# Forget gate's rows written into their operands in place, and first weights in smaller pieces, in a two-layer decoder trunk

## The chip, the cores and the metric

The kernel runs on one core of a Trainium2 chip. The metric is the device time of one execution in microseconds (us), as the median of several runs. The core's engines have their own instruction queues and work side by side: TensorE (PE in the rows), VectorE (DVE), ScalarE (ACT), GpSimd (POOL) and SyncE (SP), which only issues DMAs here.

## The reference

An input x of 256 tokens by 1024 features passes through two layers. All weights are float32 in memory.

```python
for layer in range(2):
    x = x + 0.5 * swiglu(rms_norm(x, norm_ffn1[layer]), ffn1 weights)      # 1024 -> 2816 -> 1024
    xn = rms_norm(x, norm_mix[layer])
    mixed = mix_stick_moba(xn, ...) if layer == 0 else mix_forget_dilated(xn, ...)
    x = x + mixed @ w_out[layer]
    x = x + 0.5 * swiglu(rms_norm(x, norm_ffn2[layer]), ffn2 weights)

def swiglu(x, w_gate, w_up, w_down):
    return (silu(x @ w_gate) * (x @ w_up)) @ w_down

def mix_forget_dilated(xn, w_in, b_f, ...):
    proj = xn @ w_in                       # q, k, v for 16 heads of 64, and 8 columns for the forget gate
    log_f = log_sigmoid(proj[..., 3072:] + b_f)
    # heads 0 to 7: q, k normed; logits = q k^T / 8 + c_i - c_j with c = cumsum(log_f); causal softmax; times v
    # heads 8 to 15: q, k normed and rotated; softmax over a dilated window of earlier keys; times v
```

## The kernel before

**Precision.** Every weight matrix is split in two after it is loaded: `hi` is a cast to fp32r on ACT, `lo` the rest, a subtraction on VectorE. Activations are split in the same way, so that each product takes three matmuls (hi by hi, hi by lo, lo by hi).

**Loading.** `unit` does this for 1 MB (or 768 KB) of weights. It takes one of the three buffers of the pool `raw`, lets SP issue the DMA, and writes two halves of hi and lo. A raw buffer comes free when the `lo` of both halves is done. SP's DMAs go in order: one that waits for a buffer holds those behind it. The first two units, the first 2 MB of the gate's weights, are loaded in two DMAs of 512 KB each, and x's second tile of 128 tokens is loaded between the two units.

**Opening.** x (two tiles of 128 tokens), the identity and the three vectors of RMS gains are loaded; TensorE transposes the gains (line 200) and x (`tt`); VectorE multiplies x by the gains (`xg`), ACT and VectorE split it into `xt`. Then come the gate's matmuls (`acc`, tokens in two tiles: 24 matmuls of 512 columns each per tile) and the up matrix's (`z`). GpSimd issues small DMAs for the head gains (`hg`) at the start.

**Mixing of layer 1.** `forget` computes the forget gate. It has the operands `ck` and `cq`, which carry the cumulated log gate as four extra rows of the second head group's product, beside rows of ones. It takes raw buffers for `wf`, `cl` (8 x 4 x 256: the two parts of c and of -c) and `rows` (zeros, ones, and the copies of `cl` by eight GpSimd DMAs), which two casts on GpSimd turn into `ck` and `cq`. At the same time the first group (dilated heads) runs its steps: `z` logits, `t` the softmax (maximum `mx` and scaling `t` on VectorE, exponential on ACT), `tt` transposes, `pT` their copies, one on VectorE and one on ACT, and `o` outputs. Between these, TensorE projects the second group's q, k and v; k1 and v1 below are the units of its k and v. `qn` are normed q or k; `rp` is the power -1/2 of a mean square (`ms`, or `hss` for heads) on GpSimd; `diag` is the identity times rp, which TensorE multiplies by ones.

**Order.** TensorE's order is written by hand: the projections are the main program and a small planner (`Weave`) inserts the other tasks by its own clock. The other engines' orders are made by the scheduler, save instructions that `keep_in_program_order` pins.

Of the kernel before, what the change touches and what calls it, by code (L numbers as in the profile page):

```python
# [16 lines left out]
P = 128  # L17
# [56 lines left out]
def bcast_rows(ap, offset, n):  # L74
    return bass.AP(tensor=ap.tensor, offset=ap.offset + offset, ap=[[0, P], [1, n]])
# [37 lines left out]
def trunk(ctx, tc, a, out):  # L113
# [69 lines left out]
    def load_x(t):  # L183
        for h in range(2):
            sl = slice(h * 512, (h + 1) * 512)
            nc.sync.dma_start(x[t][:, sl], a["x"][0, t * P:(t + 1) * P, sl])
# [5 lines left out]
        c0 = (2 * n + layer) * KT  # L192
        return gains_t[:, c0:c0 + KT]

    def load_gains():
        rows = raw_p.tile([6 * KT, P], F32, tag="raw", name="grows")
        for i, n in enumerate(("norm_ffn1", "norm_mix", "norm_ffn2")):
            nc.scalar.dma_start(rows[2 * KT * i:2 * KT * (i + 1)], a[n].rearrange("l (k p) -> (l k) p", p=P))
        tb = acc()
        nc.tensor.transpose(tb[:, :6 * KT], rows, ident[:6 * KT, :6 * KT])  # L200
        nc.vector.tensor_copy(gains_t[:, :6 * KT], tb[:, :6 * KT])

    identb = const.tile([P, P], BF, name="identb")
    negb = const.tile([P, 3, P], BF, name="negb")
# [28 lines left out]
    def unit(src, shape):  # L233

        w = raw_p.tile([P, *shape], F32, tag="raw", name=nm("raw"))
        n = shape[0] // 2
        if first_units:
            for i in range(2):
                nc.sync.dma_start(w[:, i * n:(i + 1) * n], src[:, i * n:(i + 1) * n])
            first_units.pop()()  # L240
        else:
            nc.sync.dma_start(w, src)
        parts = []
        for i in range(2):
            wi = w[:, i * n:(i + 1) * n]
            hi = spl_p.tile([P, n, shape[1]], F32R, tag="hi", name=nm("hi"))
            lo = spl_p.tile([P, n, shape[1]], F32R, tag="lo", name=nm("lo"))
            nc.scalar.copy(hi, wi)  # L248
            nc.vector.tensor_sub(lo, wi, hi.bitcast(F32))  # L249
            parts.append((hi, lo))  # L250
        return lambda k: tuple(v[:, k % n] for v in parts[k // n])

    def col_units(src, c0, width):
# [167 lines left out]
    def head_gain(src, rope, scale, i=0):  # L421

        if not rope:
            gp = hgp.tile([P, 16], F32, name=nm("hg"))[:, 0:1]
            for j in range(2):
                nc.gpsimd.dma_start(gp[j * HD:(j + 1) * HD], src.rearrange("o d -> d o"))
            if scale != 1.0:
                nc.gpsimd.tensor_scalar(gp, gp, scale, 0.0, op0=ALU.mult, op1=ALU.add)
            return gp
        g = hgp.tile([P, HD], F32, tag=f"g{i}", name=nm("hg"))  # L430
        nc.gpsimd.dma_start(g, bcast_rows(src, 0, HD))
        if scale != 1.0:
            nc.gpsimd.tensor_scalar(g, g, scale, 0.0, op0=ALU.mult, op1=ALU.add)
        gc = hgp.tile([P, 2, HD], F32, tag=f"gc{i}", name=nm("gc"))
        gs = hgp.tile([P, 2, HD], F32, tag=f"gs{i}", name=nm("gs"))
        cc = cv("cc").rearrange("p (t d) -> p t d", d=HD)
        ss = cv("ss").rearrange("p (t d) -> p t d", d=HD)
        for t in range(2):
            nc.gpsimd.tensor_mul(gc[:, t], cc[:, t], g)
            half_swap(lambda u, v: nc.gpsimd.tensor_mul(gs[:, t, u], ss[:, t, u], g[:, v]))  # L440
        return gc, gs

    def mix_gains(layer):

# [9 lines left out]
    def _mix(mp, layer, xt, gains, done):  # L454
# [55 lines left out]
        def forget():  # L510

            ck = mp.tile([P, 4, SEQ], F32R, name="ck")
            cq = mp.tile([P, 4, SEQ], F32R, name="cq")
            wf = raw_p.tile([P, KT, P], F32, tag="raw", name="wf")
            nc.gpsimd.memset(wf, 0.0)
            nc.scalar.dma_start(wf[:, :, 0:8], w[:, 3072:3080].rearrange("(k p) n -> p k n", p=P))
            bf = mp.tile([8, 224], F32, name="bf")[:, 0:1]
            nc.scalar.dma_start(bf, a["b_f"].rearrange("o h -> h o"))
            wfh = spl_p.tile([P, KT, P], F32R, tag="hi", name="wfh")
            wfl = spl_p.tile([P, KT, P], F32R, tag="lo", name="wfl")  # L520
            nc.scalar.copy(wfh, wf)
            nc.vector.tensor_sub(wfl, wf, wfh.bitcast(F32))
            pe.join(*xt.rdone)
            ps = acc()
            for k in range(KT):
                mm(ps[:, :SEQ], wfh[:, k], xt.hi[:, k], k == 0, False)
                mm(ps[:, :SEQ], wfh[:, k], xt.lo[:, k], False, False)
                mm(ps[:, :SEQ], wfl[:, k], xt.hi[:, k], False, k == KT - 1)

            def rest():  # L530
                y = mp.tile([8, SEQ], F32, tag="t1", bufs=4, name="lgy")
                e = mp.tile([8, SEQ], F32, tag="t1", bufs=4, name="lge")
                nc.vector.tensor_mul(y, ps[:8, :SEQ], xt.rb[:8])
                nc.vector.tensor_scalar(y, y, bf, None, op0=ALU.add)
                nc.scalar.activation(e, y, AF.Abs)
                nc.scalar.activation(e, e, AF.Exp, scale=-1.0)
                nc.scalar.activation(e, e, AF.Ln, bias=1.0)
                nc.vector.scalar_tensor_tensor(y, y, 0.0, e, op0=ALU.min, op1=ALU.subtract)
                yield LEAD_F
                tb = acc()  # L540
                for t in range(2):
                    nc.tensor.transpose(tb[:, 8 * t:8 * t + 8], y[:, t * P:(t + 1) * P], ident[:8, :8])
                lg = mp.tile([P, 2, 16], F32, name="lg")[:, :, 0:8]
                nc.vector.tensor_copy(lg, tb[:, 0:16].rearrange("p (t h) -> p t h", h=8))
                yield 1.0
                tb = acc()
                mm(tb[:8, 0:P], lg[:, 0], cv("le"), True)
                mm(tb[:8, P:SEQ], lg[:, 1], cv("le"), False)
                mm(tb[:8, P:SEQ], lg[:, 0], ones, False)
                ch = mp.tile([8, SEQ], F32R, tag="t1", bufs=4, name="ch")  # L550
                cl = raw_p.tile([8, 4, SEQ], F32, tag="raw", name="cl")
                nc.vector.tensor_copy(ch, tb[:8, :SEQ])
                nc.vector.tensor_copy(cl[:, 2], ch.bitcast(F32))
                nc.vector.tensor_sub(cl[:, 3], tb[:8, :SEQ], cl[:, 2])
                nc.vector.tensor_scalar_mul(cl[:, 0:2], cl[:, 2:4], -1.0)

                rows = raw_p.tile([P, 2, 4, SEQ], F32, tag="raw", name="rows")
                nc.gpsimd.memset(rows, 0.0)
                for s in range(2):
                    b0 = s * HD  # L560
                    nc.gpsimd.memset(rows[b0:b0 + 4], 1.0)
                    for i in range(2):
                        for j in range(2):
                            nc.gpsimd.dma_start(rows[b0 + 2 * i + j:b0 + 2 * i + j + 1, i],
                                              cl[s::2, 2 * i + j])
                for i, dst in enumerate((ck, cq)):
                    nc.gpsimd.tensor_copy(dst, rows[:, i])

            return (ck, cq), [pe.spawn(rest())]

# [169 lines left out]
        row_gemm(second.lhs, a["w_out"][layer], ca, 2, 2, lambda t, h, ps: done(t, h, ps, 1.0))  # L740


    load_x(0)
    nc.scalar.dma_start(ident, a["consts"][:, 0:P])
    load_gains()
    xt = Normed(gain(0, 0))

    def second_tile():
# [11 lines left out]
    for layer in range(2):  # L760
        nxt = Normed(gain(1, layer), True)
        gains = []

        def between():
            if layer == 0:
                load_consts()
            gains.extend(mix_gains(layer))

        ffn(layer, a["ffn1_w_gate"], a["ffn1_w_up"], a["ffn1_w_down"], xt, nxt.start, between)
        xt = nxt  # L770
        nxt = Normed(gain(2, layer))
# [29 lines left out]
```

## Time and profile before

| | before |
|---|---|
| time, median of 3 runs | 1043.26 us (1041.93 to 1043.9) |
| time of the profiled execution | 1043.78 us |
| its span, first to last instruction | 1042.0 us |
| TensorE busy (matmul) | 1004.4 us, 96% |
| VectorE busy | 604.9 us, 58% |
| ScalarE busy | 498.9 us, 48% |
| GpSimd busy | 98.3 us, 9% |
| read from memory | 173.99 MB |

The span is the time that the trace covers; the execution's own time is 1.78 us longer. Shares are of the span. Matmuls are pipelined, so two that run back to back overlap in the rows: a matmul's place is its start.

### The profile page before, as it was taken

The page shows a single profiled execution, that of the slowest core. Times are in us where ns is not written, and L with a number is a line of the kernel's source. Part 1 is how long each engine was busy: PE and PEld are TensorE (multiplying, and loading weights), DVE is VectorE, ACT ScalarE, POOL GpSimd, SP SyncE. Part 2 cuts the span into 40 slices and gives each one's busy share as a digit, 9 for nine tenths or more (in the row PEclk, how much of TensorE's full clock was granted, in tenths as well). Part 3 has the DMA queues.
Part 4 walks back from the last instruction along what each step waited for, and adds up shares of the span by engine and source line. Part 5 has one row for each costly group of instructions (what it writes and reads, how often), then busy time and mean ns, then how long its engine had stood idle before and what let it go on. Part 6 is the DMA issues. An engine that isn't in the chain of part 4 may idle for free.

```text
span 1042.0 us, 13509 instructions
## 1 busy us (share of the span) xinstructions
PE 1004.4 (96%) x5409; PEld 834.6 (80%) x5409; DVE 604.9 (58%) x794; ACT 498.9 (48%) x666; POOL 98.3 (9%) x109
## 2 busy tenths in 40 slices
PE   5999999999999999999999999999968899999998
PEld 3888988879777888988788899887746678889986
DVE  5654564588676554554655455458576755545541
ACT  6644554455665444543545345346344545435530
POOL 5000000064000000000000000005461000000000
PEclk9999999999999999999999999999988999999999
DMA  9664655464233654665455546534144424545631
GB/s 308 228 208 123 219 206 199 146 217 162 84 123 122 213 178 124 211 235 182 164 187 178 175 156 244 185 120 156 41 163 162 162 82 163 202 150 180 235 122 40
DMA packets 81871, 175.95 MB, mean 169 GB/s; under 512 B 4480, under 2 KB 21200, under 8 KB 81808
## 3 DMA queue, kind: packets, MB, share of 16 engines
q1 hardware_dynamic: 80000, 174.80, 49.4%
q8 instruction: 42, 0.69, 0.3%
q0 software_dynamic: 512, 0.17, 0.2%
q10 hardware_dynamic: 1296, 0.12, 0.1%
q14 instruction: 21, 0.17, 0.0%
HBM read 173.99 MB, written 1.05 MB: 168 GB/s over the span
## 4 chain that ended last, share of the span: by engine, by line
PE 89%; DVE 5%; DMA 2%; ACT 2%; issue 1%; POOL 0%; ACTq 0%; POOLq 0%
PE acc L149 55%; PE z L149 24%; PE o L149 6%; DVE lo L249 3%; PE tt L165 3%; ACT hi L248 1%; PE tt L149 1%; DMA raw<-in_ffn_w_up 1%; DMA x<-in_x 1%; DMA raw<-in_w_in_cd 1%; DVE xg L291 0%; ACT t L670 0%; DVE mx L664 0%; DVE t L674 0%; DMA ident<-in_consts 0%
## 5 line engine op out<-in xcount | busy, mean ns | idle before, releaser
L249 DVE TENSOR_TENSOR lo<-raw,hi 128x1024 fp32r<-128x1024 f32 (+1 forms) x344 | 403.0, 1183 | 247.2 <-ACT hi L248 235.9
L248 ACT CAST hi<-raw 128x1024 fp32r<-128x1024 f32 (+1 forms) x344 | 344.0, 1011 | 301.6 <-PE z L149 130.8
L149 PE MATMUL acc<-hi,xt 128*128 128x512 f32 (+1 forms) x1088 | 346.4, 388 | 5.7 <-ACT xt L292 2.5
L149 PEld LDWEIGHTS acc<-hi,xt 128*128 128x128 f32 x1088 | 205.6, 191 | 46.4 <-DVE xt L293 4.4
L149 PE MATMUL z<-hi,xt 128*128 128x512 f32 (+1 forms) x768 | 226.4, 371 | 0.0
L149 PE MATMUL acc<-lo,xt 128*128 128x512 f32 (+1 forms) x544 | 208.3, 383 | 1.8 <-DVE lo L249 1.8
L149 PEld LDWEIGHTS z<-hi,xt 128*128 128x128 f32 x768 | 142.4, 188 | 19.9
L149 PE MATMUL z<-lo,xt 128*128 128x512 f32 (+1 forms) x384 | 142.3, 371 | 0.0
L149 PEld LDWEIGHTS acc<-lo,xt 128*128 128x128 f32 x544 | 104.1, 191 | 17.7 <-DVE lo L249 2.1
L149 PE MATMUL acc<-hi,hh 128*128 128x512 f32 x264 | 103.5, 392 | 0.0
L149 PE MATMUL acc<-hi,hl 128*128 128x512 f32 x264 | 102.9, 390 | 0.0
L149 PE MATMUL acc<-lo,hh 128*128 128x512 f32 x264 | 102.8, 389 | 0.0
L227 POOL TENSOR_TENSOR rp<-ms,mhalf 128x1 f32<-128x1 f32 (+1 forms) x24 | 36.7, 1527 | 637.1 <-DVE ms L225 637.0
L149 PEld LDWEIGHTS z<-lo,xt 128*128 128x128 f32 x384 | 72.1, 188 | 10.0
L392 DVE TENSOR_TENSOR h<-z,sg 128x512 f32<-128x512 f32 (+1 forms) x48 | 30.9, 643 | 53.1 <-PE z L149 53.1
L149 PEld LDWEIGHTS acc<-hi,hl 128*128 128x128 f32 x264 | 49.5, 188 | 10.4
L149 PEld LDWEIGHTS acc<-hi,hh 128*128 128x128 f32 x264 | 49.5, 188 | 10.4
L149 PEld LDWEIGHTS acc<-lo,hh 128*128 128x128 f32 x264 | 49.6, 188 | 10.0
L388 ACT ACTIVATE sg<-acc,rp 128x512 f32<-128x512 f32 (+1 forms) x48 | 31.4, 654 | 42.2 <-PE acc L149 41.6
L261 ACT CAST hh<-tt 128x512 fp32r<-128x512 f32 (+1 forms) x48 | 26.5, 552 | 44.9 <-PE tt L165 24.7
L262 DVE TENSOR_TENSOR hl<-tt,hh 128x512 fp32r<-128x512 f32 (+1 forms) x48 | 31.0, 647 | 20.3 <-ACT hh L261 19.7
L149 PE MATMUL o<-hi,hh 128*128 128x512 f32 x88 | 34.4, 391 | 0.0
(144 smaller groups left out, 806.6 us busy)
## 6 DMA issues: line engine op xcount, KB each, us to landing
raw<-in_ffn_w_down SPq DMA_DIRECT2D x44, 1024.0 KB, 5.0
raw<-in_ffn_w_up SPq DMA_DIRECT2D x32, 1024.0 KB, 5.1
raw<-in_ffn_w_gate SPq DMA_DIRECT2D x30, 1024.0 KB, 5.1
raw<-in_ffn_w_gate SPq DMA_DIRECT2D x16, 768.0 KB, 4.5
raw<-in_ffn_w_up SPq DMA_DIRECT2D x16, 768.0 KB, 4.4
raw<-in_w_in_ab SPq DMA_DIRECT2D x12, 1024.0 KB, 5.2
raw<-in_w_in_cd SPq DMA_DIRECT2D x12, 1024.0 KB, 5.2
raw<-in_w_out SPq DMA_DIRECT2D x8, 1024.0 KB, 5.1
```

The lines of the kernel that those rows point to most:

```text
L149: nc.tensor.matmul(o, lhsT, rhs, start=start, stop=stop, skip_group_check=True)
L165: nc.tensor.transpose(tb[:, b, n * HP:(n + 1) * HP], src[r, j * P:(j + 1) * P], ident[r, r])
L227: nc.gpsimd.tensor_tensor(r, m, mhalf[:, :width], op=ALU.pow)
L248: nc.scalar.copy(hi, wi)
L249: nc.vector.tensor_sub(lo, wi, hi.bitcast(F32))
L261: nc.scalar.copy(halves(hi), v)
L262: nc.vector.tensor_sub(halves(lo), v, halves(hi).bitcast(F32))
L388: nc.scalar.activation(sg[t][:, :n], pg[:, :n], AF.Silu, scale=xt.r[t])
L392: nc.vector.tensor_mul(hs[t][:, :n], pu[:, :n], sg[t][:, :n])
```

## The change

The loading of the start is written anew: the identity goes first, on SP's queue; ACT's first instruction is a load of its function table; only the gains of the first norm are loaded at the start, those of the other two just before w_down of layer 0. The first two units are loaded in four DMAs of 256 KB each, and their hi and lo are made in pieces of that size; x's second tile is loaded behind both. The head gains' DMAs are pinned in program order. In `forget`, `ck` and `cq` are set to zeros and ones by GpSimd at its start, `cl` has a buffer of its own, and the eight DMAs write straight into `ck` and `cq`; `rows`, the two casts and one copy are gone.

```diff
-    def load_gains():
-        rows = raw_p.tile([6 * KT, P], F32, tag="raw", name="grows")
-        for i, n in enumerate(("norm_ffn1", "norm_mix", "norm_ffn2")):
+    def load_gains(names):
+        rows = raw_p.tile([2 * KT * len(names), P], F32, tag="raw", name=nm("grows"))
+        for i, (n, name) in enumerate(names):
...
-        if first_units:
-            for i in range(2):
-                nc.sync.dma_start(w[:, i * n:(i + 1) * n], src[:, i * n:(i + 1) * n])
-            first_units.pop()()
-        else:
-            nc.sync.dma_start(w, src)
+        pieces = 4 if first_units else 1
+        for i in range(pieces):
+            sl = slice(i * shape[0] // pieces, (i + 1) * shape[0] // pieces)
+            nc.sync.dma_start(w[:, sl], src[:, sl])
...
-            nc.scalar.copy(hi, wi)
-            nc.vector.tensor_sub(lo, wi, hi.bitcast(F32))
+            m = min(n, 2 * n // pieces)
+            for j in range(0, n, m):
+                nc.scalar.copy(hi[:, j:j + m], w[:, i * n + j:i * n + j + m])
+                nc.vector.tensor_sub(lo[:, j:j + m], w[:, i * n + j:i * n + j + m], hi[:, j:j + m].bitcast(F32))
             parts.append((hi, lo))
+        if first_units:
+            first_units.pop()()
...
-        nc.gpsimd.dma_start(g, bcast_rows(src, 0, HD))
+        tc.keep_in_program_order(nc.gpsimd.dma_start(g, bcast_rows(src, 0, HD)))
...
+            for dst in (ck, cq):
+                nc.gpsimd.memset(dst.bitcast(F32), 0.0)
+                for s in range(2):
+                    nc.gpsimd.memset(dst[s * HD:s * HD + 4].bitcast(F32), 1.0)
             wf = raw_p.tile([P, KT, P], F32, tag="raw", name="wf")
...
-                ch = mp.tile([8, SEQ], F32R, tag="t1", bufs=4, name="ch")
-                cl = raw_p.tile([8, 4, SEQ], F32, tag="raw", name="cl")
-                nc.vector.tensor_copy(ch, tb[:8, :SEQ])
-                nc.vector.tensor_copy(cl[:, 2], ch.bitcast(F32))
-                nc.vector.tensor_sub(cl[:, 3], tb[:8, :SEQ], cl[:, 2])
-                nc.vector.tensor_scalar_mul(cl[:, 0:2], cl[:, 2:4], -1.0)
-
-                rows = raw_p.tile([P, 2, 4, SEQ], F32, tag="raw", name="rows")
-                nc.gpsimd.memset(rows, 0.0)
+
+                cl = mp.tile([8, 4, SEQ], F32R, name="cl")
+                nc.vector.tensor_copy(cl[:, 2], tb[:8, :SEQ])
+                nc.vector.tensor_sub(cl[:, 3], tb[:8, :SEQ], cl[:, 2].bitcast(F32))
+                nc.vector.tensor_scalar_mul(cl[:, 0:2], cl[:, 2:4].bitcast(F32), -1.0)
                 for s in range(2):
                     b0 = s * HD
-                    nc.gpsimd.memset(rows[b0:b0 + 4], 1.0)
-                    for i in range(2):
+                    for i, dst in enumerate((ck, cq)):
                         for j in range(2):
-                            nc.gpsimd.dma_start(rows[b0 + 2 * i + j:b0 + 2 * i + j + 1, i],
-                                              cl[s::2, 2 * i + j])
-                for i, dst in enumerate((ck, cq)):
-                    nc.gpsimd.tensor_copy(dst, rows[:, i])
+                            nc.gpsimd.dma_start(dst[b0 + 2 * i + j:b0 + 2 * i + j + 1].bitcast(F32),
+                                                cl[s::2, 2 * i + j].bitcast(F32))
...
+    nc.scalar.preload_act_table_set("silu_and_others")
+    nc.sync.dma_start(ident, a["consts"][:, 0:P])
     load_x(0)
-    nc.scalar.dma_start(ident, a["consts"][:, 0:P])
-    load_gains()
+    load_gains([(0, "norm_ffn1")])
...
-    first_units.extend([lambda: None, second_tile])
+    first_units.extend([second_tile, lambda: None])
...
             if layer == 0:
                 load_consts()
+                load_gains([(1, "norm_mix"), (2, "norm_ffn2")])
```

VectorE's first rows, before (x_81 is x's first tile, x_82 its second; raw_111 and raw_124 the first two units):

```order
L225 TENSOR_SCALAR ms_167<-ss_165 128x1
L201 COPY gains_t<-acc_98 128x48
L249 TENSOR_TENSOR lo_117<-raw_111,hi_116 128x1024
L291 TENSOR_TENSOR xg_152<-tt_135,gains_t 128x512
L291 TENSOR_TENSOR xg_156<-tt_135,gains_t 128x512
L249 TENSOR_TENSOR lo_121<-raw_111,hi_120 128x1024
L225 TENSOR_SCALAR ms_208<-ss_206 128x1
L293 TENSOR_TENSOR xt_102<-xg_152,xt_101 128x4x128
L293 TENSOR_TENSOR xt_102<-xg_156,xt_101 128x4x128
L249 TENSOR_TENSOR lo_128<-raw_124,hi_127 128x1024
L249 TENSOR_TENSOR lo_132<-raw_124,hi_131 128x1024
```

The same rows of the changed kernel (raw_110 and raw_127 are the first two units):

```order
L202 COPY gains_t<-acc_97 128x16
L226 TENSOR_SCALAR ms_178<-ss_176 128x1
L293 TENSOR_TENSOR xg_163<-tt_146,gains_t 128x512
L293 TENSOR_TENSOR xg_167<-tt_146,gains_t 128x512
L249 TENSOR_TENSOR lo_116<-raw_110,hi_115 128x512 x2
L295 TENSOR_TENSOR xt_101<-xg_163,xt_100 128x4x128
L249 TENSOR_TENSOR lo_122<-raw_110,hi_121 128x512
L295 TENSOR_TENSOR xt_101<-xg_167,xt_100 128x4x128
L249 TENSOR_TENSOR lo_122<-raw_110,hi_121 128x512
L249 TENSOR_TENSOR lo_133<-raw_127,hi_132 128x512 x2
L249 TENSOR_TENSOR lo_139<-raw_127,hi_138 128x512 x2
```

The gains' copy and xg stand ahead of every lo now, and lo goes in eight pieces with the xt between them.

ACT in the mixing of layer 1, before, from the square (`sq`) of q1's first tile on (raw_6436 and raw_6446 hold the two halves of k1's weights):

```order
L486 ACTIVATE sq_6325<-acc_6244,rp_5797 128x512
L666 ACTIVATE t_19_6361<-z_6349,mx_6359 128x128
L666 ACTIVATE t_20_6373<-z_6350,mx_6371 128x128
L682 COPY pT_6396<-tt_6383 128x384
L666 ACTIVATE t_19_6361<-z_6349,mx_6359 128x256
L666 ACTIVATE t_20_6373<-z_6350,mx_6371 128x256
L486 ACTIVATE sq_6460<-acc_6321,rp_5900 128x512
L248 CAST hi_6438<-raw_6436 128x1024
L248 CAST hi_6442<-raw_6436 128x1024
L248 CAST hi_6448<-raw_6446 128x1024
L248 CAST hi_6452<-raw_6446 128x1024
```

ACT of the changed kernel some rows earlier in the program, around the log-sigmoid (`lge`); raw_6451 and raw_6461 hold k1's weights, raw_6695 the first half of v1's:

```order
L248 CAST hi_6453<-raw_6451 128x1024
L248 CAST hi_6457<-raw_6451 128x1024
L248 CAST hi_6463<-raw_6461 128x1024
L506 ACTIVATE kT_5980<-tt_6189 128x4x128
L470 ACTIVATE v_3_6202<-acc_6167,rp_5917 128x512
L248 CAST hi_6467<-raw_6461 128x1024
L248 CAST hi_6697<-raw_6695 128x1024
L541 ACTIVATE lge<-lgy 8x256
```

k1's four casts, which stood behind the softmax of the first group's second step, now stand ahead of the log-sigmoid, and a cast of v1 with them.

GpSimd between the two diag tiles of the mixing norm of layer 1, before:

```order
L227 TENSOR_TENSOR rp_5797<-ms_5795,mhalf 128x1
L305 TENSOR_TENSOR diag_5799<-ident,rp_5797 128x128
L515 MEMSET wf 128x1024
L227 TENSOR_TENSOR rp_5900<-ms_5898,mhalf 128x1
L305 TENSOR_TENSOR diag_5902<-ident,rp_5900 128x128
```

and of the changed kernel:

```order
L228 TENSOR_TENSOR rp_5814<-ms_5812,mhalf 128x1
L307 TENSOR_TENSOR diag_5816<-ident,rp_5814 128x128
L517 MEMSET ck 128x1024
L517 MEMSET cq 128x1024
L519 MEMSET ck 4x1024 x2
L519 MEMSET cq 4x1024 x2
L521 MEMSET wf 128x1024
L228 TENSOR_TENSOR rp_5917<-ms_5915,mhalf 128x1
L307 TENSOR_TENSOR diag_5919<-ident,rp_5917 128x128
```

Six memsets have come in ahead of wf's and of the second tile's rp and diag.

## Rows read from the trace of the kernel before

**Rows 1.** The page's busy times: engine, us, share of span, instructions.

```profile
PE 1004.4 (96%) x5409; PEld 834.6 (80%) x5409; DVE 604.9 (58%) x794; ACT 498.9 (48%) x666; POOL 98.3 (9%) x109
```

**Rows 2.** TensorE's waits over the span: total us, times, longest.

```profile
PE acc L200 <- DMA x<-in_x: 9.7, 1, 9.7
```

**Rows 3.** Timeline of the opening: start, us, engine, line, operation, [idle before <-releaser].

```profile
2.14 0.45 ACTq L198 DMA_DIRECT2D grows<-in_norm_ffn  x1
...
9.67 0.31 PE L200 MATMUL acc<-ident,grows 48*128 48x48 f32 x1 [9.67 <-DMA x<-in_x]
...
11.27 1.28 DVE L291 TENSOR_TENSOR xg<-tt,gains_t 128x512 f32<-128x512 f32 x2
...
12.47 1.22 DVE L249 TENSOR_TENSOR lo<-raw,hi 128x1024 fp32r<-128x1024 f32 x1
...
13.40 0.80 PE L149 MATMUL acc<-hi,xt 128*128 128x512 f32 x1 [2.55 <-ACT xt L292]
...
21.67 1.28 ACT L388 ACT_TABLE_LOAD   x1 [0.50 <-PE acc L149]
...
27.64 0.39 PE L149 MATMUL z<-hi,xt 128*128 128x512 f32 x1
27.87 0.39 PE L149 MATMUL z<-lo,xt 128*128 128x512 f32 x1
```

**Rows 4.** DMA view, 0 to 30 us: GB/s in 40 slices; then KB, us to landing.

```profile
GB/s 0 0 109 238 379 326 107 40 192 377 392 367 331 385 396 391 377 385 385 388 410 388 385 393 382 366 393 390 388 208 104 208 396 412 352 63 3 68 180 377
...
x<-in_x SPq DMA_DIRECT2D x4, 256.0 KB, 5.3
...
ident<-in_consts ACTq DMA_DIRECT2D x1, 64.0 KB, 3.3
grows<-in_norm_ffn ACTq DMA_DIRECT2D x2, 8.0 KB, 7.4
```

**Rows 5.** Windows in layer 1's mixing; the sum is of four with PEclk 0.50.

```profile
740.00:750.00 10.00, 10.00 (x62) 7.92 (x61) 4.64 (x20) 4.12 (x9) 0.00 (x0) 1.00 0.01 2
757.00:798.31 41.31, 27.94 (x155) 20.29 (x154) 30.36 (x68) 20.43 (x30) 14.76 (x14) 0.79 0.60 204
...
791.49:798.31 6.82, 6.26 (x29) 4.47 (x29) 2.96 (x9) 2.10 (x3) 0.30 (x1) 0.50 0.71 279
sum 17.05, PE 15.89 PEld 12.18 DVE 12.00 ACT 6.54 POOL 5.77; mean PE 3.97 PEld 3.04 DVE 3.00 ACT 1.64 POOL 1.44
```

**Rows 6.** TensorE's timeline, 755 to 800 us: the five rows that waited.

```profile
758.90 0.49 PE L149 MATMUL acc<-hi,xt 128*128 128x512 f32 x1 [1.77 <-ACT hi L248]
761.16 0.79 PE L149 MATMUL acc<-lo,xt 128*128 128x512 f32 x1 [1.76 <-DVE lo L249]
...
771.23 0.69 PE L165 MATMUL tt<-ident,qn 64*128 64x64 f32 x8 [4.21 <-ACT pT L682]
...
783.40 0.46 PE L165 MATMUL tt<-ident,qn 64*128 64x64 f32 x8 [2.69 <-ACT pT L682]
...
792.05 1.11 PE L165 MATMUL tt<-ident,t 64*128 64x64 f32 x12 [2.94 <-DVE t L674]
```

**Rows 7.** Timelines of VectorE and ACT in the same stretch.

```profile
758.64 0.53 DVE L674 TENSOR_SCALAR t<-t,l 128x128 f32<-128x128 f32 x2
...
767.89 1.99 ACT L248 CAST hi<-raw 128x1024 fp32r<-128x1024 f32 x2 [8.10 <-DMA raw<-in_w_in_cd]
```

**Rows 8.** Timelines of GpSimd, 690 to 770 us, and of TensorE at 711.

```profile
695.25 0.55 POOL L227 TENSOR_TENSOR rp<-ms,mhalf 128x1 f32<-128x1 f32 x1 [172.92 <-DVE ms L225]
...
706.30 0.95 POOL L515 MEMSET wf<- 128x1024 f32 x1 [10.02 <-DMA bf<-in_b_f]
707.58 2.66 POOL L227 TENSOR_TENSOR rp<-ms,mhalf 128x1 f32<-128x1 f32 x1 [0.33 <-DVE ms L225]
...
754.48 3.69 POOL L561 MEMSET rows<- 4x2048 f32 x2
...
711.01 0.38 PE L149 MATMUL acc<-diag,ones 128*128 128x128 f32 x2
```

More of the change, by code (lines that the diff above doesn't have):

```diff
@@ L193, in gain @@
         return gains_t[:, c0:c0 + KT]
-    def load_gains():
-        rows = raw_p.tile([6 * KT, P], F32, tag="raw", name="grows")
-        for i, n in enumerate(("norm_ffn1", "norm_mix", "norm_ffn2")):
-            nc.scalar.dma_start(rows[2 * KT * i:2 * KT * (i + 1)], a[n].rearrange("l (k p) -> (l k) p", p=P))
+    def load_gains(names):
+        rows = raw_p.tile([2 * KT * len(names), P], F32, tag="raw", name=nm("grows"))
+        for i, (n, name) in enumerate(names):
+            nc.scalar.dma_start(rows[2 * KT * i:2 * KT * (i + 1)], a[name].rearrange("l (k p) -> (l k) p", p=P))
+        m, c0 = 2 * KT * len(names), 2 * KT * names[0][0]
         tb = acc()
-        nc.tensor.transpose(tb[:, :6 * KT], rows, ident[:6 * KT, :6 * KT])
-        nc.vector.tensor_copy(gains_t[:, :6 * KT], tb[:, :6 * KT])
+        nc.tensor.transpose(tb[:, :m], rows, ident[:m, :m])
+        nc.vector.tensor_copy(gains_t[:, c0:c0 + m], tb[:, :m])
     identb = const.tile([P, P], BF, name="identb")
@@ L236, in unit @@
         n = shape[0] // 2
-        if first_units:
-            for i in range(2):
-                nc.sync.dma_start(w[:, i * n:(i + 1) * n], src[:, i * n:(i + 1) * n])
-            first_units.pop()()
-        else:
-            nc.sync.dma_start(w, src)
+        pieces = 4 if first_units else 1
+        for i in range(pieces):
+            sl = slice(i * shape[0] // pieces, (i + 1) * shape[0] // pieces)
+            nc.sync.dma_start(w[:, sl], src[:, sl])
         parts = []
         for i in range(2):
-            wi = w[:, i * n:(i + 1) * n]
             hi = spl_p.tile([P, n, shape[1]], F32R, tag="hi", name=nm("hi"))
             lo = spl_p.tile([P, n, shape[1]], F32R, tag="lo", name=nm("lo"))
-            nc.scalar.copy(hi, wi)
-            nc.vector.tensor_sub(lo, wi, hi.bitcast(F32))
+            m = min(n, 2 * n // pieces)
+            for j in range(0, n, m):
+                nc.scalar.copy(hi[:, j:j + m], w[:, i * n + j:i * n + j + m])
+                nc.vector.tensor_sub(lo[:, j:j + m], w[:, i * n + j:i * n + j + m], hi[:, j:j + m].bitcast(F32))
             parts.append((hi, lo))
+        if first_units:
+            first_units.pop()()
         return lambda k: tuple(v[:, k % n] for v in parts[k // n])
@@ L425, in head_gain @@
             for j in range(2):
-                nc.gpsimd.dma_start(gp[j * HD:(j + 1) * HD], src.rearrange("o d -> d o"))
+                tc.keep_in_program_order(nc.gpsimd.dma_start(gp[j * HD:(j + 1) * HD], src.rearrange("o d -> d o")))
             if scale != 1.0:
```

## The prediction

> **What bounds the kernel now.** I read the page first: TensorE is busy for 1004.4 us, 96% of the span [rows 1]. So only some 38 us of idle TensorE, and what a low clock costs it, can be won; work taken off another engine counts only where TensorE waits for it. The list of TensorE's waits names the largest: 9.7 us at line 200, the transpose of the gains at the start [rows 2]. The other long ones lie close together in the timeline, in layer 1's mixing (below). The change touches both places.
>
> The opening comes from the timeline [rows 3]. The transposes of the gains start at 9.67 although x was asked for first. What they wait for is the gain rows: the third DMA of them is issued at 2.14 and, by the DMA view, these take about 7.4 us to land, while the identity on the same queue took 3.3 [rows 4]. The inferred releaser says x, which took 5.3 from an earlier issue; it was long there. In the same answer the transfer rate falls to 107 and 40 GB/s in the slices from 4.5 to 6 us (40 slices over 30 us), beside some 390 later; that is when the six small DMAs that GpSimd issues for the head gains are under way. From 9.67 a chain runs: xg at 11.27, first weight matmul at 13.40, first matmul of z at 27.64 [rows 3]. From there the matmuls follow 0.23 apart (27.64, 27.87), with no wait among the list's larger ones before the mixing, so what z's start gains is kept.
>
> The second place: from 757 to 798.31 TensorE is busy 27.94 of 41.31 us [rows 5]. Five waits make up the rest: 1.77, 1.76, 4.21, 2.69 and 2.94 [rows 6], 13.4 together. After such waits the granted clock is 0.50 (the lower level, 1.2 GHz) for stretches with 15.89 us of busy TensorE [rows 5]; at the higher level that is half, so 7.9 is lost to the clock. Together 21.3 us, over 20.0 of work. The cause lies in the buffers: cl and rows (whose memsets run around 754 [rows 8]) hold two of the three raw buffers, so the weights of k1's second half and v1 come late: ACT, idle for 8.10, can make the second half's hi only at 767.89 when its DMA lands, and the pT that TensorE wants stands behind those casts [rows 7]. From 740 to 750, just before, VectorE is busy 4.64 of 10 and the DMA share is 0.01 [rows 5]: room for the same work earlier.
>
> **The opening, part by part.** Gone from the start: two of three gain DMAs, six head-gain DMAs of GpSimd (now in order, far later, when nothing waits: their products are used tens of us afterwards) and the table load of 1.28 at 21.67 [rows 3], which moves to ACT's first slot, where it lies beside x's landing. But the one gain DMA left is issued behind it, at some 0.7 + 1.3 = 2.0. Landing: between 3.3 us (the identity) and 7.4 us (gains before) later [rows 4], so 5.3 to 9.4. I take 5.5: the queue that slowed it is gone and it is nearest to the identity, 16 rows from memory. The Trainium skill ("DMA: Bandwidth & Descriptors", section "Queues, rings and completion order") says that each DMA engine takes turns between the queues that have work, a packet at a time; by that the gains would not stand behind 2 MB of weights, T would be 5.3 and the opening worth -5.4, where the gains' own row gives 9.4 and -1.3. The identity's 3.3 agrees with the rule and the gains' 7.4, by itself, does not.
>
> From the gains' landing T: xg begins 11.27 - 9.67 = 1.6 later and two take 1.28 [rows 3], so T + 2.9. Then VectorE does, in its new order, eight lo pieces (128x512, half of 1.22, so 0.61 [rows 3]) and two xt of 0.64: T + 9.1. For x's second tile: two xg 1.28, an ms 0.15, an xt 0.64, two lo of 1.22 for the up weights, an xt 0.64: T + 14.2. The second token tile's last 12 matmuls need that xt: 12 x 0.227 = 2.7 (27.64 to 27.87 [rows 3]), so z starts at T + 16.9. With T = 5.5 that is 22.4, against 27.64: **-5.2**. With T = 9.4 it is -1.3; with 5.0, -5.7. Weights are not late: 2.6 MB at 390 GB/s lie before x's second tile, so it lands at some 9 to 12 us, and VectorE reaches it at 14.6.
>
> The other gains now come in layer 0 just before w_down. Their buffer waits for the mask constants; ACT is idle there, and w_down has two buffers until then. A lo more stands ahead of one h, and TensorE gets one more transpose: **+0.4** (0 to 1.2, one lo).
>
> **The mixing of layer 1.** With cl in a tile of its own, and the rows copied by DMA straight into ck and cq, no raw buffer is taken there. In the new order ACT casts k1's four halves and one of v1 before the log-sigmoid, and VectorE follows; their buffers are freed by splits done before 730, so the loads land before 745. The waits of 1.77 and 1.76 go entirely. Also gone: 128x2048 and two 4x2048 memsets (3.69 for the pair [rows 8]), two CASTs on GpSimd, one small copy on VectorE.
>
> The three later waits shrink or stay, and a new one comes, because TensorE arrives earlier while VectorE has more in hand. I laid the new rows of VectorE and ACT end to end with the old durations. The scaling of t that pair 1's transposes need ended at 758.64 + 0.53 = 759.2 [rows 7]. Now about 1.0 of shift, two lo (2.4), an hss (0.69), two mx (0.5) come ahead of it, less the copy (0.4): some 763.4. TensorE, with 12 matmuls (2.7), a z of 1.2 and no wait from 757, is there at 760.9: a wait of 2.5 to 2.9 that wasn't there; I take 2.8. In the same way the two waits for pT give 1.4 and 0.9, the next for t 3.0 (three lo ahead of it), and 0.8 goes in small ones. Sum 8.9 in place of 13.4. Two of them are near 3 us, the kind after which the clock fell for 3.41 us: 2 x 1.7 = 3.4 in place of 7.9. New length 20.0 + 8.9 + 3.4 = 32.3 against 41.3: **-9.0**. Bounds: with every wait gone -21; with as many waits as before except the first two, and the same clock, -3.5. I stay near the walk: -5 to -13. What comes behind 800 is not touched.
>
> **A new wait.** GpSimd now has six memsets (128x1024 twice, 4x1024 four times) before wf's, in order, between the gains' diag tiles. They wait for the last matmul of FFN1, about 702.3. By the pair of 4x2048, 3.69, one of 4x1024 is 0.92, and wf's 128x1024 took 0.95 [rows 8]: 7 x 0.93 = 6.5, to 708.9, where before wf's memset started at 706.30 and rp at 707.58. Behind them rp (2.66) and diag (0.40): to about 712.0. TensorE's ones-by-diag matmul stood at 711.01 [rows 8]: **+1.1** (0, if rp takes 0.55 as at 695.25, to 2). The Trainium skill ("GPSIMD Engine Reference", section "8. Key points") warns that GpSimd shares its memory interfaces with VectorE, which contends when it reads two inputs. wf's memset took 0.95 beside a VectorE that is busy throughout, so a memset doesn't show it; rp's 2.66 against 0.55 would fit. If memsets suffered like rp, the wait would be longer by some us.
>
> **Sum.** -5.2 - 9.0 + 1.1 + 0.4 = -12.7. The profiled execution took 1043.78, 0.52 above the median, so 1031.1 for it and **1030.6** for the median 1043.26. Differences within 0.2% (2.1 us) I call no change.
>
> **Rivals.** (1) The gains land no earlier (T = 9.4): for it, they go behind the table load and beside four pieces already queued; against, GpSimd's DMAs are gone. 1043.26 - 1.3 - 9.0 + 1.5 = 1034.5. (2) VectorE is the bound in the mixing: it is busy 30.36 of 41.31 there [rows 5], and only 0.4 of its work is removed. Waits stay as long as the three were, clock too: -3.5, so 1043.26 - 5.2 - 3.5 + 1.5 = 1036.1. Against it: 5 of the lo halves move ahead of 757. (3) **Slower**: the shorter waits follow one another so closely that the clock stays low over the whole mixing stretch, as it did from 791.49 to 798.31 [rows 5]. With 20.0 of work at half clock, 40 + 8.9 against 41.3 gives +7.6; with -5.2 + 1.5: +3.9, so 1047.2. It decides once 16 of the 20 us of work run low (28.9 + 16 = 45, which eats the opening's gain). Against it: the other three low stretches ended after 3.41 us. (4) The change does not do what it says: T late and the mixing's waits only renamed, 1043.26 - 1.3 - 2 + 1.5 = 1041.5.
>
> **Numbers.** Forecast 0.60 (its own range 1026 to 1034.3), rival 1 0.13, rival 2 0.15, rival 3 0.06, rival 4 0.06. The range reaches down to -18 (opening -5.7, mixing -13, no new wait) and up past rival 2: 1025 to 1038. It leaves out rivals 3 and 4 and some of the edges. Faster 0.88, no change 0.06, slower 0.06.
>
> **What would show it.** Right: line 201's transpose at 5 to 6; z's first matmul near 22.4; one table load before the first square; k1's hi and lo casts before lge; no wait on hi or lo near 757; two waits near 3 us between 755 and 785 (less the shift), each with 3.41 us at 0.50; a wait on diag of about 1 us. Wrong: gains landing at 9; a clock of 0.50 for most of the mixing; waits of 4 us there again; memsets of 1.8 us each.

## The result, and the profile after

The changed kernel takes 1029.43 us (median of 4 runs, 1028.47 to 1030.1) against 1043.53 for the kernel before beside it: a ratio of 0.9867, with a 95% interval of 0.985 to 0.9884, so 14.1 us or 1.3% faster. The forecast was 1030.6, a change of -12.7; the measured time lies 1.2 us below it, within its range. The profiled execution took 1029.01, 14.8 below that of before, with a span of 1027.2.

The page, busy times (engine, us, share of the span), as in [rows 1]:

```profile
PE 1003.0 (98%) x5410; PEld 833.3 (81%) x5410; DVE 603.3 (59%) x798; ACT 497.7 (48%) x669; POOL 87.9 (9%) x110
```

TensorE does the same work within a span that is 14.8 us shorter. Its waits over the span (us in total, times, longest), the first six of nine, against [rows 2]:

```profile
PE tt L165 <- DVE t L673: 4.7, 4, 1.6
PE z L149 <- ACT t L669: 3.9, 4, 2.3
PE acc L201 <- DMA ident<-in_consts: 2.9, 1, 2.9
PE z L149 <- ACT kT L506: 2.1, 2, 1.4
PE acc L149 <- ACT xt L294: 2.1, 1, 2.1
PE acc L149 <- DVE xt L295: 1.8, 4, 0.7
```

The 9.7 us wait for the gains is now 2.9, and no wait is longer than that. The timeline of the opening (start, us, engine, line, operation), against [rows 3]:

```profile
0.72 1.28 ACT L742 ACT_TABLE_LOAD   x1 [0.72 <-PEq L790]
...
0.76 0.40 ACTq L198 DMA_DIRECT2D grows<-in_norm_ffn  x1
...
2.85 0.28 PE L201 MATMUL acc<-ident,grows 16*128 16x16 f32 x1 [2.85 <-DMA ident<-in_consts]
...
4.27 1.36 PE L165 MATMUL tt<-ident,x 64*128 64x64 f32 x16 [1.14 <-DMA x<-in_x]
...
6.04 1.12 ACT L248 CAST hi<-raw 128x512 fp32r<-128x512 f32 x2
6.17 0.15 DVE L226 TENSOR_SCALAR ms<-ss 128x1 f32<-128x1 f32 x1 [2.82 <-ACT junk L302]
6.25 1.29 DVE L293 TENSOR_TENSOR xg<-tt,gains_t 128x512 f32<-128x512 f32 x2
...
7.07 0.61 ACT L294 CAST xt<-xg 128x512 fp32r<-128x512 f32 x1
...
7.74 0.80 PE L149 MATMUL acc<-hi,xt 128*128 128x512 f32 x1 [2.10 <-ACT xt L294]
...
9.40 1.22 PE L149 MATMUL acc<-hi,xt 128*128 128x512 f32 x2 [0.41 <-DVE xt L295]
...
18.41 0.69 DVE L295 TENSOR_TENSOR xt<-xg,xt 128x512 fp32r<-128x512 f32 x1
...
21.98 0.39 PE L149 MATMUL z<-hi,xt 128*128 128x512 f32 x1
```

The gains' transpose went from 9.67 to 2.85, z's first matmul from 27.64 to 21.98, and the opening has no table load behind 2.00. One profile fixes z's place only to some 1.4 us: in seven profiles with this opening (the change twice, and the runs below on the opening alone, the held buffers and the two orders) z's first matmul stands between 21.98 and 23.34; with the opening of before it stands at 27.64, and at 28.28 in the run of the forget part alone. The DMA view of the same 30 us (GB/s in 40 slices; KB and us to landing), against [rows 4]:

```profile
GB/s 0 0 92 238 306 352 325 333 339 371 369 358 391 380 382 404 410 401 412 401 385 382 388 391 393 390 380 380 382 393 399 126 180 385 396 336 128 158 401 412
...
ident<-in_consts SPq DMA_DIRECT2D x1, 64.0 KB, 2.1
grows<-in_norm_ffn ACTq DMA_DIRECT2D x1, 8.0 KB, 1.9
```

The dip to 107 and 40 GB/s between 4.5 and 6 us is gone (325 and 333 in its place), and the gains land 1.9 us after their issue.

In layer 1's mixing TensorE's waits are these (timeline, 738 to 784 us), against [rows 6]:

```profile
741.54 0.92 PE L149 MATMUL z<-kT,qT 64*128 64x256 f32 x8 [1.35 <-ACT kT L506]
...
758.21 0.51 PE L165 MATMUL tt<-ident,t 64*128 64x64 f32 x6 [1.27 <-DVE t L673]
...
761.30 0.69 PE L165 MATMUL tt<-ident,qn 64*128 64x64 f32 x8 [0.24 <-ACT pT L681]
...
772.34 0.46 PE L165 MATMUL tt<-ident,qn 64*128 64x64 f32 x8 [0.76 <-ACT pT L681]
...
778.34 0.60 PE L165 MATMUL tt<-ident,t 64*128 64x64 f32 x6 [1.59 <-DVE t L673]
```

The waits for hi and lo are gone, the 4.21 and 2.69 for pT are 0.24 and 0.76, the 2.94 for t is 1.59; 1.27 for t is new, and so is the 1.35 for kT. The windows at the lower clock (columns as in [rows 5]):

```profile
759.43:766.26 6.83, 6.59 (x30) 4.74 (x28) 3.77 (x16) 2.10 (x4) 0.42 (x1) 0.50 0.02 4
779.91:783.32 3.41, 3.41 (x9) 2.38 (x8) 1.35 (x3) 1.82 (x3) 0.39 (x1) 0.50 0.75 285
```

10.00 us of busy TensorE run at 1.2 GHz there, against 15.89.

Matmul by matmul, in the order of the program, the new kernel is ahead by 5.7 us at z's first matmul, 5.5 at layer 0's w_down, 4.85 from layer 0's mixing norm (210.66 before, 205.81 after) up to layer 1's mixing, 3.4 at the row at 741.54, and 15.1 once the mixing of the first group is done. The rest of the program keeps that to within 0.3 us.

### The profile page after: what moved, and what is told of

Same layout as the page of the kernel before. It is cut to its first block, busy times and chain, and to the rows that moved or that the text cites. A ratio compares the mean times of both kernels' runs of the same rounds, so it can differ in the third digit from the quotient of the medians.

```text
span 1027.2 us, 13525 instructions
## 1 busy us (share of the span) xinstructions
PE 1003.0 (98%) x5410; PEld 833.3 (81%) x5410; DVE 603.3 (59%) x798; ACT 497.7 (48%) x669; POOL 87.9 (9%) x110
## 4 chain that ended last, share of the span: by engine, by line
PE 88%; DVE 6%; ACT 2%; issue 1%; POOL 1%; DMA 1%; SPq 0%; ACTq 0%; DVEq 0%; POOLq 0%
PE acc L149 54%; PE z L149 25%; PE o L149 6%; DVE lo L249 3%; PE tt L165 3%; ACT hi L248 1%; PE tt L149 1%; POOL rp L228 1%; POOL sq L498 1%; DMA raw<-in_w_in_ab 1%; DVE mx L663 0%; ACT t L669 0%; DMA x<-in_x 0%; DVE qn L493 0%; DVE xg L293 0%
## 5 line engine op out<-in xcount | busy, mean ns | idle before, releaser
L249 DVE TENSOR_TENSOR lo<-raw,hi 128x1024 fp32r<-128x1024 f32 (+2 forms) x348 | 403.4, 1171 | 240.5 <-ACT hi L248 229.8
L248 ACT CAST hi<-raw 128x1024 fp32r<-128x1024 f32 (+2 forms) x348 | 344.6, 1001 | 293.8 <-PE z L149 124.8
L228 POOL TENSOR_TENSOR rp<-ms,mhalf 128x1 f32<-128x1 f32 (+1 forms) x24 | 31.9, 1328 | 618.8 <-DVE ms L226 618.7
```

The source lines that it names most:

```text
L228: nc.gpsimd.tensor_tensor(r, m, mhalf[:, :width], op=ALU.pow)
L248: nc.scalar.copy(hi[:, j:j + m], w[:, i * n + j:i * n + j + m])
L249: nc.vector.tensor_sub(lo[:, j:j + m], w[:, i * n + j:i * n + j + m], hi[:, j:j + m].bitcast(F32))
```

## The experiments

All were timed against the kernel before in interleaved rounds; the ratio with its interval decides.

| run | median us | ratio to before | 95% interval |
|---|---|---|---|
| the change | 1029.43 | 0.9867 | 0.985 to 0.9884 |
| the change, again | 1028.89 | 0.9859 | 0.9845 to 0.9872 |
| forget part alone | 1033.9 | 0.991 | 0.9896 to 0.9925 |
| opening alone | 1039.69 | 0.9964 | 0.9951 to 0.9977 |
| two raw buffers held | 1036.77 | 0.9933 | 0.9909 to 0.9958 |
| head gains first | 1031.03 | 0.9887 | 0.987 to 0.9903 |
| two pieces | 1030.46 | 0.9873 | 0.986 to 0.9887 |
| three gains first | 1031.17 | 0.9881 | 0.9867 to 0.9894 |
| both first | 1034.31 | 0.9907 | 0.9892 to 0.9922 |
| before, head gains late | 1041.28 | 0.9976 | 0.9967 to 0.9985 |
| xg ahead of ms | 1029.23 | 0.986 | 0.9846 to 0.9874 |
| log-sigmoid behind kT | 1024.78 | 0.9818 | 0.9802 to 0.9833 |
| both orders | 1025.0 | 0.9817 | 0.9801 to 0.9833 |

**Each part alone.** The function `forget` is exchanged whole between the two kernels:

```diff
-                cl = raw_p.tile([8, 4, SEQ], F32, tag="raw", name="cl")
+                cl = mp.tile([8, 4, SEQ], F32R, name="cl")
...
```

The first run makes this and the rest of `forget`'s edits in the kernel before; the second takes them back in the changed kernel.

> The kernel before with the forget part alone. The theory that the two parts add up, and that the mixing of layer 1 is worth about 10 us in the changed kernel's trace, expects 1033 to 1035 us (9 to 10 below 1043.5). The rival, that the mixing gains only because TensorE comes to it in another phase, expects 1038 or more.

> The changed kernel with the forget gate of before. If the parts add up, the opening is worth 5 to 5.5 us and the time is 1038 to 1039. The rival, that the earlier opening is eaten by later waits, expects 1041 or more.

The forget part gives 9.4 us (by its ratio), as expected; the opening 3.8 (2.4 to 5.1), under the 5 to 5.5 expected. Together 13.2, against 13.9 and 14.7 in the two timings of the change: they add up within their intervals. The opening's shortfall shows in its profile: z starts at 22.75, which is 4.9 ahead of before, and 3.6 is left behind the mixing norm of layer 0. The phase in which TensorE arrives at layer 1's mixing doesn't matter much: there the run keeps waits of 1.8, 1.8, 6.6 for pT and 4.5 for t, and its lead of 3.6 before them is 3.5 after them.

**The buffers or the work?** Two raw buffers are taken again, but not the work that went with them:

```diff
-                cl = mp.tile([8, 4, SEQ], F32R, name="cl")
+                cl = raw_p.tile([8, 4, SEQ], F32R, tag="raw", name="cl")
+                rows = raw_p.tile([P, 2, 4, SEQ], F32, tag="raw", name="rows")
+                held = mp.tile([P, 1], F32, name="held")
+                nc.gpsimd.memset(rows[:, 0, 0, 0:1], 0.0)
...
+                for dst in (ck, cq):
+                    nc.gpsimd.tensor_add(held, rows[:, 0, 0, 0:1], dst[:, 0, 0:1].bitcast(F32))
```

> The changed kernel, but cl lies in a raw buffer again and a second raw buffer is taken (one column set) until the rows' DMAs have landed; the large memsets, the casts and the copy stay away. Two columns of adds on GpSimd are added, whose output nothing uses. If the gain of the mixing is that of the two buffers, most of it goes: 1036 to 1041. If it is the work removed from GpSimd and VectorE, the time stays at 1029 to 1031.

1036.77, with runs spread from 1032.99 to 1038.46: about 7 us are lost in the median. The profile is of the longest of the four runs, and it has 10.24 us at the lower clock from 823 us on where the change has 3.41 from 821, so it shows more loss than the median. TensorE's timeline of this run, 740 to 800 us, has the waits of before again:

```profile
755.01 0.50 PE L149 MATMUL acc<-hi,xt 128*128 128x512 f32 x1 [1.77 <-ACT hi L248]
756.60 0.50 PE L149 MATMUL acc<-lo,xt 128*128 128x512 f32 x1 [1.09 <-DVE lo L249]
...
765.79 0.69 PE L165 MATMUL tt<-ident,qn 64*128 64x64 f32 x8 [4.71 <-ACT pT L686]
...
781.72 0.46 PE L165 MATMUL tt<-ident,qn 64*128 64x64 f32 x8 [2.79 <-ACT pT L686]
```

And ACT's timeline shows the row that stands ahead of pT, as in [rows 7]:

```profile
762.86 1.99 ACT L248 CAST hi<-raw 128x1024 fp32r<-128x1024 f32 x2 [6.95 <-DMA raw<-in_w_in_cd]
```

So the borrowed buffers cost most of it. What is left of the mixing's gain beside the opening alone (0.9933 against 0.9964, some 3 us, with intervals that overlap slightly) may be the work that is gone; no run separates it.

**What made the gains late?** The forecast had GpSimd's head-gain DMAs. One kernel brings these back to the start (the two pins are taken off), one brings the other two norms' gains back, one brings back both:

```diff
-            tc.keep_in_program_order(nc.gpsimd.dma_start(g, bcast_rows(src, 0, HD)))
+            nc.gpsimd.dma_start(g, bcast_rows(src, 0, HD))
...
-    load_gains([(0, "norm_ffn1")])
+    load_gains([(0, "norm_ffn1"), (1, "norm_mix"), (2, "norm_ffn2")])
```

> The changed kernel, with the head gains' DMAs no longer pinned, so GpSimd issues six of them at the start again. If they slowed the gains and x in the opening, the gains land at 5 us or later instead of 2.65, x later too, and the time is 1031 to 1034. If the gains were late only because three DMAs stood in ACT's queue behind the identity, the gains land by 3 us and the time is 1029 to 1030.

> The changed kernel, but all three norms' gains are loaded at the start, by three DMAs in ACT's queue, and transposed together; GpSimd's DMAs stay late. If the gains were late before because three small DMAs stood in that queue while the weights were already under way, the third lands at 5 us or later, the transpose comes there instead of 2.85, and the time is 1 to 3 us longer. If a gain DMA lands within 2 us of its issue whatever its number, the transpose is at about 3.5 to 4 and the time is the same, since x lands at 4.9.

> The changed kernel with all three gains' DMAs at the start and GpSimd's six head-gain DMAs there too, as before. Each alone put the gains' transpose at 4.83 and at 2.96. If the two act together (gains and head gains in the engines' way while the weights queue), it comes at 7 us or later and the time is 1033 to 1035. If each acts for itself, it comes at about 5 and the time is 1031 to 1033.

And the kernel before, with nothing but the head gains' DMAs pinned:

> The kernel before with one thing changed: the head gains' DMAs are pinned in program order, so none is left at the start. If they made the gains late, the gains' transpose moves from 9.67 to between 4.5 and 6 us and the time falls by 2 to 4, to 1040 to 1041.5. If the gains were late from their place in ACT's queue, behind the identity and beside weights, the transpose stays at 8.5 or later and the time at 1042.5 to 1044.

The transposes of the gains, in the timelines of the four, in that order:

```profile
2.96 0.28 PE L201 MATMUL acc<-ident,grows 16*128 16x16 f32 x1 [2.96 <-DMA ident<-in_consts]
...
8.04 0.62 ACT L248 CAST hi<-raw 128x512 fp32r<-128x512 f32 x1 [1.09 <-DMA raw<-in_ffn_w_gate]
```

```profile
4.83 0.31 PE L201 MATMUL acc<-ident,grows 48*128 48x48 f32 x1 [4.83 <-DMA grows<-in_norm_ffn]
```

```profile
7.30 0.31 PE L201 MATMUL acc<-ident,grows 48*128 48x48 f32 x1 [7.30 <-DMA grows<-in_norm_ffn]
```

```profile
7.64 0.31 PE L200 MATMUL acc<-ident,grows 48*128 48x48 f32 x1 [7.64 <-DMA grows<-in_norm_ffn]
```

With the change's 2.85 and before's 9.67 this is a table, z's first matmul beside it. Each z is that of one profile, so it is known to some 1.4 us:

| gains first | head gains first | transpose | z |
|---|---|---|---|
| one | none (the change, two profiles) | 2.85, 2.85 | 21.98, 23.34 |
| one | six | 2.96 | 24.66 |
| three | none | 4.83 | 25.53 |
| three | six | 7.30 | 28.40 |
| three, in before's order | none | 7.64 | 25.41 |
| three, in before's order | six (before) | 9.67 | 27.64 |

The head gains hardly delay a lone gain DMA: by the DMA view it lands 2.0 us after its issue at 0.76, when GpSimd has issued two of the six and begins the third. They delay what comes behind: the first hi cast waits for weights until 8.04 where it began at 6.04 and, in the change's second profile, at 7.37. The dip in the transfer rate is theirs too. These are the rates of the same 30 us with the head gains first:

```profile
GB/s 0 0 84 206 344 183 93 79 191 200 374 356 205 265 402 396 402 410 399 393 385 396 404 391 393 390 388 377 390 390 339 221 366 401 339 178 208 396 393 341
```

From 4.5 to 6 us they are 93 and 79; with three gains and no head gains they are 320 and 306. Three gains in place of one cost 2.0 us of the transpose, and the head gains 2.5 more once there are three.

By the expectations, the lone gain's transpose fits the second case of its run (gains by 3 us) and the time the first (1031.03); the three gains' 4.83 and 1031.17 come near their first case; with both back, 7.30 and 1034.31 are the first case, in which the two act together. The times of the first two, 1031.03 and 1031.17 beside 1028.89 and 1029.43, have intervals that overlap the change's slightly; that of both, 1034.31, lies clear of it. With both back nothing of the opening's gain is left: the ratio is 0.9907, that of the forget part alone 0.991, and z stands at 28.40 against 27.64 and 28.28 with the opening of before. So with the small DMAs there the new order (identity first, smaller pieces, early table load) shows no gain: the opening's gain hangs on their leaving. In the kernel before, the head gains alone are worth 2.5 us (1041.28), as the expectation's first case says, though the transpose moved only to 7.64, which neither case expected.

**Smaller pieces.**

```diff
-        pieces = 4 if first_units else 1
+        pieces = 2 if first_units else 1
```

> The changed kernel with its first two units loaded in two DMAs of 512 KB each, and split in halves, as before. If VectorE's chain after the gains sets the opening, 256 KB pieces matter only by the first lo standing between xg and xt: z starts up to 1 us later and the time is 0 to 1 us longer. The rival, that the first matmul waits for weights to land, expects 1.5 us or more.

1030.46 against 1028.89 for the change beside it; the intervals overlap, so whether the time is longer stays open. The profile speaks for the rival: xg starts at 6.17 as in the change, but ACT waits for the first 512 KB until 8.08, the xt that TensorE needs stands behind that cast, and the first matmul comes at 9.70 (7.74 and 9.24 in the change):

```profile
8.08 1.04 ACT L248 CAST hi<-raw 128x1024 fp32r<-128x1024 f32 x1 [2.03 <-DMA raw<-in_ffn_w_gate]
...
9.70 0.80 PE L149 MATMUL acc<-hi,xt 128*128 128x512 f32 x1 [4.15 <-ACT xt L294]
```

z starts at 24.59 there. The change run again is this:

> The changed kernel once more, as the measure for the three that run beside it: 1028 to 1030 us, a ratio of about 0.9867 to the kernel before.

In its profile the first hi cast waits for weights, the first matmul is at 9.24 and z at 23.34; so "weights are not late" doesn't hold in every execution, for the first pieces. ACT's timeline:

```profile
7.37 1.30 ACT L248 CAST hi<-raw 128x512 fp32r<-128x512 f32 x2 [1.37 <-DMA raw<-in_ffn_w_gate]
8.57 0.61 ACT L294 CAST xt<-xg 128x512 fp32r<-128x512 f32 x1
```

**The two waits that the change left.** xg stands at 6.25 behind a mean square, at 6.17, that nothing needs yet. And ACT's kT stands behind the log-sigmoid. ACT's timeline of the changed kernel:

```profile
740.59 0.41 ACT L543 ACTIVATE lge<-lge 8x256 f32<-8x256 f32 x1
740.91 0.57 ACT L506 ACTIVATE kT<-tt 128x512 f32<-128x512 f32 x1
```

Both orders are moved, together and one by one. `i` is the mean square; the yield of 3.0 stands ahead of the log-sigmoid; the pin on kT also holds for the other qT and kT:

```diff
-        nc.vector.tensor_scalar(m, ss, 1.0 / n, EPS, op0=ALU.mult, op1=ALU.add)
+        i = nc.vector.tensor_scalar(m, ss, 1.0 / n, EPS, op0=ALU.mult, op1=ALU.add)
+        if seen["ms"] == 1:
+            tc.keep_in_program_order(i)
...
-                nc.scalar.activation(halves(qT[:, :, t * P:(t + 1) * P]), transposes(o)[0], AF.Copy,
-                                     scale=1.0 if rope else g)
+                tc.keep_in_program_order(nc.scalar.activation(halves(qT[:, :, t * P:(t + 1) * P]), transposes(o)[0], AF.Copy,
+                                     scale=1.0 if rope else g))
...
+                yield 3.0
...
-                nc.scalar.activation(e, y, AF.Abs)
+                tc.keep_in_program_order(nc.scalar.activation(e, y, AF.Abs))
...
-                yield LEAD_F
+                yield LEAD_F - 3.0
```

> The changed kernel with two orders moved: the mean square of x's first tile behind xg on VectorE, and the log-sigmoid of the forget gate behind the last kT on ACT. The trace shows xg waiting 0.6 us for that mean square, and TensorE 1.35 us for kT. If both are as they look, the time is 1 to 2 us below the changed kernel's beside it. The rival: kT's wait only moves to the next one (t or pT), and the gain is 0.5 or less.

> The changed kernel with only the mean square of x's first tile behind xg. The pair of orders gave 3.9 us. The trace of the pair shows xg where x's second half had landed, so this alone: 0 to 0.7 us below 1029.2. The rival, that the opening's order gave most of it: 2 or more.

> The changed kernel with only the log-sigmoid behind the last kT. If kT's wait and the clock after it carry the pair's gain: 1025 to 1026.5. If the two share it: 1027 to 1028.

The mean square is worth nothing (1029.23): xg starts at 6.10 instead of 6.11 to 6.25, for x lands later in that profile (its transposes start at 4.71, against 4.27). The log-sigmoid's place alone gives 4.1 us (4.3 by the ratios): 1024.78, and its interval lies clear of the change's; the pair is the same, 1025.0, a gain of 3.9 where 1 to 2 were expected. ACT's timeline of the kernel with kT alone:

```profile
739.24 0.60 ACT L506 ACTIVATE kT<-tt 128x512 f32<-128x512 f32 x1 [1.49 <-PE tt L165]
...
743.64 0.40 ACT L542 ACTIVATE lge<-lgy 8x256 f32<-8x256 f32 x1
```

kT starts as soon as its transposes are done, and in that profile the row of z that waited 1.35 has no wait; TensorE's waits from 740 to 790 fall from 3.1 for t, 1.4 for kT and 1.0 for pT to 1.9, none and 1.1, and 0.7 for another. Those add up to 1.8, and 3.41 us at the lower clock in place of 10.24 to some 3 more; of that, 1.7 is given back at 812, where 6.83 stand against 3.41. But the repeat of the change had 3.41 too. The window from 740 to 800 us, in the repeat and in the pair (columns as in [rows 5]):

```profile
740.00:800.00 60.00, 53.68 (x343) 39.69 (x342) 43.44 (x119) 31.01 (x56) 11.81 (x12) 0.97 0.40 139
740.00:800.00 60.00, 55.51 (x348) 41.29 (x344) 44.02 (x123) 32.15 (x58) 11.80 (x12) 0.97 0.40 135
```

The granted clock is the same in the two, and the pair's span is 2.8 us shorter (1023.2 against 1026.0), 0.6 of which it has before layer 1's mixing. So some 2 us of the gain need no clock; how much of the rest is the clock's stays open.

## Why the prediction was right, step by step

**The opening** (-5.2 forecast, -5.7 in the profile, 3.8 in its own run). That the small DMAs held the opening back was right; that the size came out was luck, from three wrong steps. "Landing: ... I take 5.5" was too late: 2.65 (0.76 + 1.9). "Issued behind" the table load was wrong, the DMA goes out at 0.76 while the load runs from 0.72 to 2.00. But the chain doesn't start at the gains then: x lands for the transposes at 4.27, and VectorE waits for the mean square until 6.17. And the chain's end is not VectorE's. From xg on VectorE goes as worked out: its last xt is done at 19.10 (18.41 + 0.69), 12.85 behind xg's start, where T + 14.2 less T + 1.6 are 12.6. But TensorE doesn't wait for it: after its first weight matmul its only wait is 0.41, at 9.40. So z's start is the first matmul, 7.74, and 14.24 of TensorE's own, as 13.40 and 27.64 are 14.24 apart in [rows 3], with one wait of 0.46 between. The first matmul hangs on ACT, whose xt (7.07) stands behind two hi casts; where these wait for weights, z comes later, 23.34 in the repeat. The 1.6 from the gains to xg also held a lo of 1.22 that the new order has behind xg.

The cause was only half named: "the queue that slowed it is gone" holds for weights, and for three gains, and not for one. The Trainium skill ("DMA: Bandwidth & Descriptors", section "Queues, rings and completion order") lets the engines take turns between queues, a packet at a time. The traces neither bear that out nor speak against it: the lone gains land at 2.8, before most of the head gains are issued, and the third of three, issued at 1.64 and 1.65, is there for the transpose at 4.83 without them and at 7.30 with them, a price that the rule doesn't give.

**Between** (+0.4). The lead of 5.7 shrinks at w_down, to 5.5, and by 0.6 at layer 0's mixing norm, where TensorE's wait for xt grew from 0.21 to 0.70: +0.8 in all. Why the second was longer isn't settled; it isn't there with the forget part alone, and it is there with the opening alone (a wait of 0.72).

**The new wait** (+1.1). It didn't come. GpSimd's timeline, against [rows 8]:

```profile
697.56 0.96 POOL L517 MEMSET ck<- 128x1024 f32 x1 [6.11 <-PE o L149]
...
699.35 1.93 POOL L519 MEMSET ck<- 4x1024 f32 x2
...
703.30 0.96 POOL L521 MEMSET wf<- 128x1024 f32 x1
704.22 1.19 POOL L228 TENSOR_TENSOR rp<-ms,mhalf 128x1 f32<-128x1 f32 x1
705.49 0.40 POOL L307 TENSOR_TENSOR diag<-ident,rp 128x128 f32<-128x128 f32 x1
```

The memsets are as forecast (0.96 each; from 697.56 to 704.26 is 6.7 against 6.5), but rp takes 1.19, not 2.66, so diag is done at 705.89 and TensorE's matmul comes at 706.16 without a wait. The mis-sized term is rp, whose row of before was taken as its price. The Trainium skill ("GPSIMD Engine Reference", section "8. Key points") warns that GpSimd shares its memory interfaces with VectorE and contends with instructions that read two inputs there. The memsets show no sign of it: VectorE is busy 9.13 of the 10 us from 700 on, and they take what one did before. The rows of rp agree with it: of the twelve of 128 x 1 in the kernel before, the six with none of VectorE's lo or xt beside them take 0.55 to 0.57, the six with some take 0.93 to 2.66. The 2.66 had 2.4 us of them beside it, the 1.19 of the new kernel 0.85. So rp's price was that of its place, which the memsets moved. No run separates this from other causes.

**The mixing** (-9.0). The mechanism was right, shown by the run that holds the buffers. The lead grows from 4.85 to 15.1, so -10.2, made of three terms that were off; that they nearly cancel is luck. The waits were put at 8.9; those for t and pT are 4.1 (1.27, 0.25, 0.24, 0.76, 1.59). The clock was put at 3.4; 10.00 us of busy time at half speed make 5.0, and the clock fell at 759.43, after waits of 1.27 and 0.25, and at 779.91, after one of 1.59, none of them near 3. The repeat of the change, with waits of the same size, had 3.41 us. And kT's wait of 1.35, which isn't there before, was not seen: the walk began at 757, and at 741 the change had moved casts and splits ahead of the log-sigmoid that ACT does before kT. These terms make 21.3 - 4.1 - 5.0 - 1.35 = 10.9; 0.7 of it is not in the lead. The rival of the low clock throughout, and that of VectorE as the bound with 4 us waits, didn't come about.

**The sum.** -5.7 + 0.8 + 0 - 10.2 = -15.1 in the trace (-14.8 at its end), where -12.7 was forecast; by the medians -14.1. Of the signs named, z near 22.4, the one table load, k1's casts before lge and no wait on hi or lo near 757 were seen; the transpose at 5 to 6, the two waits near 3 us and the wait on diag were not.

## What to carry to other kernels

A buffer borrowed from the weights' pool for a small job costs what the loads behind it come late by (about 7 us here), and that appears as a wait on an engine far from it: look at who holds the pool when a DMA's issue stands still. Small DMAs at the start of a kernel are not free because they are small; move those whose data is needed later. A size that comes out right doesn't show that the chain behind it is right: look in the new trace for the wait that the chain claims (TensorE had none for VectorE's last xt). After a gain like this, read the new list of waits: an order that the scheduler shifted along (the log-sigmoid ahead of kT) was worth another 4 us.

## What the runs showed of the hardware that was not expected

Two more gain DMAs of 8 KB and six head-gain DMAs of 0.2 to 32 KB together put z's start at 28.40, where it stands between 21.98 and 23.34 without them: 5.1 to 6.4 us, while the bytes are under 0.2 MB. The head gains alone make it 24.66 and the gains alone 25.53. ACT issued a DMA at 0.76 during its own table load. A memset of 4 x 1024 on GpSimd took as long as one of 128 x 1024 (1.93 for two, 0.96 for one). And two profiled executions of the same changed kernel had 10.24 and 3.41 us at the lower clock in the mixing; the one whose z started 1.36 us later ended 1.2 us earlier.
